# A third raw weight buffer from the gates to the first products, and operand sums in two column parts, in a streaming encoder step

## The chip, the cores and the metric

The kernel runs on one core of one Trainium2 chip. The metric is the device time of one execution in microseconds (us). Engines are named as in the profile: PE (TensorE, matrix products), ACT (ScalarE), DVE (VectorE), POOL (GpSimd), and SP (SyncE), which only issues DMAs. Each engine works through its own instructions in order and waits on semaphores that the others raise. The on-chip memory SBUF has 128 partitions; a tile "128 x n" has n columns on each.

## The reference

One layer on 1056 tokens (1024 prompt, 32 sample), model width 1024, in float32:

```python
h = rms_norm(x, g_mix)
q, k, v, ch, cb, cc, ga, gb = jnp.split(h @ w_in, SPLITS, axis=-1)
a = attn_core(q, k, v) @ w_attn_out                  # windowed attention
bo = (cb * causal_conv3(cc * ch)) @ w_conv_out       # gated short convolution
x = x + (jax.nn.sigmoid(ga) * a + jax.nn.sigmoid(gb) * bo) @ w_mix_out
x = x + memory_attention(rms_norm(x, g_cross) @ w_cq) @ w_co
x = x + jnp.square(jax.nn.relu(rms_norm(x, g_mlp) @ w_up)) @ w_down
y = rms_norm(x, g_final)
```

## The kernel before

Activations lie transposed, features on partitions, tokens on columns, in three chunks `CH` of 384, 384 and 288 tokens; the MLP works on two halves of `HT` = 528 tokens, each of two quarters of `QT` = 264. Every float32 product is three PE products: both operands are split into a high part (fp32r) and a rest, and hi x hi, hi x lo and lo x hi are added (`gemm`, `product`). `split` makes the high part on ACT and the rest on DVE.

**Weights.** `fetch_w` (L147) issues on SP the DMA of a 512 KB weight into a raw tile `wr`, of which there are two; `issue_w` (L158) splits it into `wh` and `wl`. In the gates a dictionary `third` is filled at pair 1 (L933) and cleared at the last pair (L936); while it is filled, each third fetch takes a further raw tile, `wr3`, out of the pool `gtop`, which is open in the gates alone.

**Weight sums.** Gates and MLP use seven products for a 2 x 2 block product instead of eight, which needs sums of weight blocks. POOL makes them in 50 pieces (`pieces`, L692): `sum_step` (L702) loads the next piece from DRAM and then adds the blocks of the piece before in four `tensor_tensor` operations (L719) and stores it to `gsum_d`, `wsum_d` or `usum_d`. Two tiles take turns: `ws` (L700, pool `W["pool"]`, one buffer) and `xacc`. Calls of `sum_step` are placed in the program's order among the attention and output-projection steps. The last piece, a part of `usum_d`, is in `ws`.

**Gates.** `gate_pair(f)` (L908), f from 1 to 7, takes four weights: w_in column 34+f, two sums of `gsum_d` (fetched as `g_sum`), and w_in column 42+f. Its products are 12 matmuls of 384 columns each (3 x 4 row blocks), and for some f a further 24 of 288 columns (`gate_c2`). The first needs only w_in 34+f; the third, `t2`, needs `g_sum` (f-1, 0); the next, `n1`, needs `g_sum` (f-1, 1).

**The stretch after the gates.** Output projections and cross attention of each chunk run as a list of 48 `fillers` (L1648 on): projections of chunk 2, then the first MLP products `up_one` (quarter by quarter, `NQ` row groups) and `up_two` (both quarters). Dictionary `at` hangs further steps behind a filler by its number (`then`, L1657). `up_one` and `up_two` put their results in tiles from `lslot` (L1262, tag `lt`, six buffers; `us`/`uh` with two each for the first three) and store them to `s1_d` and `op_d["b11"]` one step later (`put`, `flush`).

`normed(c, f)` (L1281) computes the MLP's normalised input on DVE and stores it to DRAM (`xn_d`). The operands of the second half of the products are sums of it: n3 = b12 - b22, t2 = b11 - n3, n1 = b11 - b12, n4 = b21 - t2, where the b are quarters of features by halves of tokens. Before, `open_sums` (L1233) loads the parts known by then into the tiles `comb`, `normed(2, f)` adds the columns of chunk 2 by DMA, `sums_first` and `sums_then` (L1377, L1390) compute the sums over all 528 columns into other tiles, three of the four results go by DMA from SBUF to SBUF into `comb`, and `comb_split` (L1397) splits n1, n3 and n4 there at the start of the second half (`up_start`, `up_pair`).

An order of instructions on each engine is made by a scheduler from the program's order and a timeline of its own; instructions under `pin` keep the program's order.

Of the kernel before, what the change touches and what calls it, by code (L numbers as in the profile page):

```python
# [10 lines left out]
F32 = mybir.dt.float32  # L11
# [7 lines left out]
P = 128  # L19
# [4 lines left out]
NF = 8  # L24
# [16 lines left out]
def hybrid_step(ctx: ExitStack, tc: tile.TileContext, io):  # L41
# [37 lines left out]

    ao_d = [[dram.tile([P, 2, n], F32, name=f"ao_d{c}_{kv}") for kv in range(KV)] for c, (_, n) in enumerate(CH)]  # L80
    bc_d, m1_d = spill("bc_d"), spill("m1_d")
    xn_d = [dram.tile([P, NF, HT], F32, name=f"xn_d{h}") for h in range(2)]

    op_d = {k: dram.tile([P, 16, HT], F32, name=f"{k}_d") for k in ("b11", "b21", "b22", "n1", "n3", "t2", "n4")}
    s1_d = dram.tile([P, 16, HT], F32, name="s1_d")
# [61 lines left out]
    def fetch_w():  # L147
        if third:
            third["n"] += 1
        if third and third["n"] % 3 == 0:  # L150
            raw = third["pool"].tile([P, 1024], F32, tag="wr3", name=nm("wr3"))
        else:
            raw = wp.tile([P, 1024], F32, tag="wr", bufs=2, name=nm("wr"))
        src = weight(worder[wpos[0] + len(fetched)])
        sp.dma_start(raw.rearrange("p (i c) -> p i c", i=4) if len(src.shape) == 3 else raw, src)
        fetched.append(raw)
# [751 lines left out]
    def gate_pair(f):  # L908
# [109 lines left out]
    def after_gates():  # L1018
        nonlocal m_cm, mpool, cr_cm, cr
        assert not pieces and "new" not in W  # L1020
        closed(x_cm)
        closed(W["cm"])
# [198 lines left out]
    def open_first():  # L1221

        closed(m_cm)
        S["l"] = ctx.enter_context(tc.tile_pool(name="first", bufs=6, reuse_waits="tile"))
        S["z"] = ctx.enter_context(tc.tile_pool(name="second", bufs=8, reuse_waits="tile"))
        for f in range(NF):
            z = zslot()
            xa[1][f] = (quarter(z, 0), quarter(z, 1))
            sp.dma_start(xa[1][f][1].bitcast(F32)[:, : CH[0][1] - QT], xn_d[0][:, f, QT : CH[0][1]])
        for name in ("w_cq", "w_co"):  # L1230
            del kept[name, 1]

    def open_sums():  # L1233
        closed(cr_cm)
        closed(Y["cm", 1])
        S["s"] = ctx.enter_context(tc.tile_pool(name="sums", bufs=8, reuse_waits="tile"))
        for kind in ("t2", "n1", "n3", "n4"):
            for k in range(4):
                comb[kind, k] = tuple(slot(S["s"], kind, HT) for _ in range(2))
        n = CH[1][0] + CH[1][1] - HT  # L1240
        for k in range(4):
            sp.dma_start(raw("t2", k), xn_d[0][:, k])
            sp.dma_start(raw("n1", k)[:, :n], xn_d[1][:, k, :n])
            sp.dma_start(raw("n3", k)[:, :n], xn_d[1][:, k + 4, :n])
            sp.dma_start(raw("n4", k), xn_d[0][:, k + 4])

    def open_late():
        closed(Y["cm"])
        L["cm"], L["pool"] = opened("late", bufs=1, reuse_waits="tile")

# [18 lines left out]
    quarters = lambda t: t.rearrange("p (q t) -> p q t", q=2)  # L1269


    def in_halves(c):
        o, n = CH[c]
        for h in range(2):
            a, b = max(o, HT * h), min(o + n, HT * h + HT)
            if a < b:
                yield h, slice(a - HT * h, b - HT * h), slice(a - o, b - o)

    xa = [[None] * NF for _ in range(2)]

    def normed(c, f):  # L1281
        t = tmp(CH[c][1])
        pin(dve.scalar_tensor_tensor(t, x1[c][f], col(G_MLP + f), R[c], op0=ALU.mult, op1=ALU.mult))
        for h, to, at in in_halves(c):
            if c < 2 or f > 3:
                sp.dma_start(xn_d[h][:, f, to], t[:, at])
# [83 lines left out]
    def second_b22():  # L1370
        for k in range(4):
            comb["b22", k] = tuple(slot(S["b"], "b22", HT) for _ in range(2))
            sp.dma_start(raw("b22", k), xn_d[1][:, k + 4])

    t2s = {}

    def sums_first(k):  # L1377
        if k == 1:
            n3, n1 = (L["pool"].tile([P, 1024], F32, tag=t, name=nm(t))[:, :HT] for t in ("s31", "s24"))
        else:  # L1380
            n3, n1 = xacc[0][:, :HT], xacc[0][:, HT:]
        t2 = t2s[k] = L["pool"].tile([P, 1024], F32, tag="wr2", bufs=2, name=nm("t2"))[:, :HT]
        pin(dve.tensor_sub(n3, raw("n1", k), raw("n3", k)))
        sp.dma_start(raw("n3", k), n3)
        pin(dve.tensor_sub(t2, raw("t2", k), n3))
        pin(dve.tensor_sub(n1, raw("t2", k), raw("n1", k)))
        sp.dma_start(raw("n1", k), n1)
        pin(act.copy(comb["t2", k][0], t2))

    def sums_then(k):  # L1390
        t2 = t2s.pop(k)
        hi, lo = comb["t2", k]
        pin(dve.tensor_sub(lo, t2, hi.bitcast(F32)))
# [79 lines left out]
    def up_pair(i):  # L1473
# [82 lines left out]
    def dslots(kind, k):  # L1556
        if KINDS.index(kind) % 2 == 0:
            tag = ("t2", "n1", "n3", "b22")[k // 4]
            pool = S["b" if tag == "b22" else "s"]
            return tuple(slot(pool, tag, HT) for _ in range(2))  # L1560
        if k < 4:
            return tuple(slot(S["s"], "n4", HT) for _ in range(2))
        if k < 8:
            return tuple(zslot() for _ in range(2))
        if k < 11:
            return tuple(lslot(F32R) for _ in range(2))
        return tuple(slot(S["h"], "H", HT) for _ in range(2))

# [10 lines left out]
    def open_down():  # L1579
        flush()  # L1580
        closed(L["cm"])
        closed(L["cm2"])
        S["h"] = ctx.enter_context(tc.tile_pool(name="hpool", bufs=10, reuse_waits="tile"))


    def cross_units(c):
# [102 lines left out]
    then(37, call(xacc_tile))  # L1689
    for f in (0, 4, 1, 5, 2, 6, 3, 7):  # L1690
        then(37, call(normed, 2, f))
# [12 lines left out]
    def up_start():  # L1704
# [267 lines left out]
```

## Time and profile before

| | us |
|---|---|
| median of three runs (lowest, highest) | 1788.23 (1781.94, 1788.44) |
| the profiled execution: time | 1787.72 |
| the profiled execution: span from first to last instruction | 1785.9 |
| PE busy in it | 1738.8 |
| POOL busy in it | 584.3 |
| granted TensorE clock, mean | 0.99 |

The profile's page gives the busy time of each engine and a picture of the span in 40 slices. Views of the trace give single stretches: instructions in order of time (start, length, engine, line, operation, output tile, input tiles), groups of equal instructions, waits with what ended them, and DMAs with the time from issue to landing. "SPq" and "POOLq" are the issuing queues. A PE matmul's shown length overlaps the next one's; the distance of two starts is what a matmul costs.

### The profile page before, as it was taken

Reading aid. Unit: us, or ns where it says so; the run is one execution under the profiler, and the core shown is the slowest. Engines: PE = TensorE matmul, PEld = TensorE weight load, DVE = VectorE, ACT = ScalarE, POOL = GpSimd, SP = SyncE. Lnnn points to the kernel's source line nnn. Section 1 sums busy time; section 2 is a strip of 40 time slices with the busy share of each in tenths; the row PEclk is TensorE's granted clock in tenths of the full one; section 3 lists DMA queues with packets and bytes.
Section 4 is the critical chain, followed back from the end, with each engine's and each line's share of the span. In section 5 each row is a group of like instructions: output and inputs, shape, how many; then the busy total and the mean of one; then the engine's idle time right before and its main releaser. Section 6 shows DMA issues by size and latency. Waiting matters only on the chain. (4 is left out here: it accounts for less than half of the span.)

```text
span 1785.9 us, 32537 instructions
## 1 busy us (share of the span) xinstructions
PE 1738.8 (97%) x12250; PEld 1717.8 (96%) x12250; DVE 1181.0 (66%) x2229; ACT 852.5 (48%) x1646; POOL 584.3 (33%) x655
## 2 busy tenths in 40 slices
PE   8999999999999999999999997998999999999998
PEld 8999999999999999999999897988999999999998
DVE  7776867868666737546676866567666686556575
ACT  8643534435345334334565754654444463333443
POOL 0025365643453444532224130014555510000121
PEclk9999999999999999999999998999999999999999
DMA  5333334334346888768765666685666686554554
GB/s 181 107 119 128 111 128 154 130 140 136 138 151 239 284 292 284 262 212 275 253 205 200 226 212 201 215 298 187 229 220 221 215 299 210 185 183 165 197 174 156
DMA packets 185820, 353.64 MB, mean 198 GB/s; under 512 B 20144, under 2 KB 104912, under 8 KB 185536
## 3 DMA queue, kind: packets, MB, share of 16 engines
q1 hardware_dynamic: 170608, 298.98, 49.3%
q0 software_dynamic: 15056, 52.60, 8.3%
q8 instruction: 96, 1.57, 0.3%
q14 instruction: 60, 0.49, 0.1%
HBM read 252.30 MB, written 94.19 MB: 194 GB/s over the span
## 5 line engine op out<-in xcount | busy, mean ns | idle before, releaser
L129 ACT CAST wh<-wr 128x1024 fp32r<-128x1024 f32 x225 | 236.3, 1050 | 435.8 <-PE acc L1758 126.2
L130 DVE TENSOR_TENSOR wl<-wr,wh 128x1024 fp32r<-128x1024 f32 x225 | 293.1, 1303 | 153.1 <-ACT wh L129 152.1
L193 PE MATMUL acc<-X,wh 128*128 128x384 f32 (+1 forms) x864 | 281.8, 326 | 7.6 <-ACT wh L129 7.6
L194 PE MATMUL acc<-X,wh 128*128 128x384 f32 (+1 forms) x864 | 279.1, 323 | 0.0
L195 PE MATMUL acc<-X,wl 128*128 128x384 f32 (+1 forms) x864 | 278.4, 322 | 0.2 <-DVE wl L130 0.2
L269 POOL TENSOR_TENSOR xacc<-xacc,ct 128x384 f32<-128x384 f32 (+1 forms) x56 | 74.6, 1335 | 404.6 <-ACT ct L267 402.7
L193 PEld LDWEIGHTS acc<-X,wh 128*128 128x128 f32 x864 | 162.9, 189 | 8.3 <-ACT wh L129 7.6
L194 PEld LDWEIGHTS acc<-X,wh 128*128 128x128 f32 x864 | 163.1, 189 | 0.6
L195 PEld LDWEIGHTS acc<-X,wl 128*128 128x128 f32 x864 | 162.8, 188 | 0.8 <-DVE wl L130 0.8
L193 PE MATMUL acc<-Y,wh 128*128 128x384 f32 (+1 forms) x432 | 139.8, 325 | 3.2 <-ACT wh L129 3.1
L195 PE MATMUL acc<-Y,wl 128*128 128x384 f32 (+1 forms) x432 | 140.0, 325 | 1.8 <-DMA wl<-wl_d 1.4
L194 PE MATMUL acc<-Y,wh 128*128 128x384 f32 (+1 forms) x432 | 140.0, 325 | 0.3 <-DVE Y L775 0.2
L1758 PE MATMUL acc<-n,wh 128*128 128x264 f32 x352 | 100.0, 284 | 0.0
L1759 PE MATMUL acc<-n,wl 128*128 128x264 f32 x352 | 100.0, 284 | 0.0
L1757 PE MATMUL acc<-n,wh 128*128 128x264 f32 x352 | 100.0, 284 | 0.0
L129 ACT CAST PTh<-pt 128x512 fp32r<-128x512 f32 (+3 forms) x94 | 46.0, 516 | 111.6 <-PE pt L582 110.8
L719 POOL TENSOR_TENSOR ws<-ws 128x256 f32<-128x256 f32 x100 | 93.5, 935 | 5.6
L719 POOL TENSOR_TENSOR xacc<-xacc 128x256 f32<-128x256 f32 x100 | 87.6, 876 | 5.6 <-DMA xacc<-in_w_in 0.3
L193 PEld LDWEIGHTS acc<-Y,wh 128*128 128x128 f32 x432 | 81.6, 189 | 3.8 <-ACT wh L129 3.4
L195 PEld LDWEIGHTS acc<-Y,wl 128*128 128x128 f32 x432 | 81.6, 189 | 2.5 <-DMA wl<-wl_d 1.7
L194 PEld LDWEIGHTS acc<-Y,wh 128*128 128x128 f32 x432 | 81.8, 189 | 0.8 <-DVE Y L775 0.8
L865 PE MATMUL acc<-n,wh 128*128 128x264 f32 x256 | 73.1, 286 | 1.4 <-DVE n L1301 1.3
(404 smaller groups left out, 5502.2 us busy)
## 6 DMA issues: line engine op xcount, KB each, us to landing
wr<-in_w_in SPq DMA_DIRECT2D x53, 512.0 KB, 4.0
wr<-in_w_up SPq DMA_DIRECT2D x52, 512.0 KB, 4.3
wr<-wsum_d SPq DMA_DIRECT2D x40, 512.0 KB, 3.4
wr<-in_w_conv_out SPq DMA_DIRECT2D x24, 512.0 KB, 4.3
wr<-in_w_mix SPq DMA_DIRECT2D x24, 512.0 KB, 4.1
wr<-in_w_down SPq DMA_DIRECT2D x24, 512.0 KB, 4.1
wl<-wl_d SPq DMA_DIRECT2D x18, 512.0 KB, 4.6
n_d<-Z SPq DMA_DIRECT2D x32, 264.0 KB, 4.1
```

Of the source, the lines that this page charges most:

```text
L129: act.copy(hi, src)
L130: dve.tensor_sub(lo, src, hi.bitcast(F32))
L193: pe.matmul(out, wh[:, a], hi, start=(k == 0), stop=False)
L194: pe.matmul(out, wh[:, a], lo, start=False, stop=False)
L195: pe.matmul(out, wl[:, a], hi, start=False, stop=(k == len(acts) - 1))
L269: pool_e.tensor_tensor(acc, acc, sq, op=ALU.add)
L719: pin(pool_e.tensor_tensor(t[:, to], t[:, x], t[:, y], op=ALU.add))
L865: pe.matmul(acc, wh[:, a], lo, start=False, stop=False, skip_group_check=True)
L1757: pe.matmul(a, wh[:, s], hi, start=(t == 0 and k == 0), stop=False, skip_group_check=True)
L1758: pe.matmul(a, wh[:, s], lo, start=False, stop=False, skip_group_check=True)
L1759: pe.matmul(a, wl[:, s], hi, start=False, stop=(t == 1 and k == 7), skip_group_check=True)
```

## The change

- The third raw buffer is now the tile `ws` of the pool `W["pool"]`, which stays open to the end; `third` is filled at gate pair 1 as before and cleared only in `open_late`, so each third fetch uses it from the gates to the first MLP products.
- `xn_d` is one tensor; `normed` of chunk 2 keeps its result in SBUF (`top`).
- The operand sums are made in two column parts: `sums_early` on the first `HA` = 240 columns (tokens of chunk 1), `sums_first` and `sums_then` on the last 288, the latter straight from the outputs of `normed`. Each part is split straight into the operand tiles; the DMAs from SBUF to SBUF and the splits of n1, n3 and n4 in the second half go.
- `lt` has four buffers instead of six, `us`/`uh` one instead of two, `H` in the down projection twelve instead of ten; seven row groups instead of six go through `up_one`; several steps hang at other fillers.

```diff
-    xn_d = [dram.tile([P, NF, HT], F32, name=f"xn_d{h}") for h in range(2)]
+    xn_d = dram.tile([P, NF, NT], F32, name="xn_d")
...
-            raw = third["pool"].tile([P, 1024], F32, tag="wr3", name=nm("wr3"))
+            raw = W["pool"].tile([P, 4, 256], F32, tag="ws", name=nm("wr3")).rearrange("p q c -> p (q c)")
...
-    W["cm"], W["pool"] = opened("wsum", bufs=1, reuse_waits="tile")
+    W["pool"] = ctx.enter_context(tc.tile_pool(name="wsum", bufs=1, reuse_waits="tile"))
...
         if f == 1:
-            third.update(n=2, pool=Y["top"])
+            assert not pieces and "new" not in W
+            third["n"] = 2
             fetch_w()
-        if f == NF - 1:
-            third.clear()
...
-        S["l"] = ctx.enter_context(tc.tile_pool(name="first", bufs=6, reuse_waits="tile"))
+        S["l"] = ctx.enter_context(tc.tile_pool(name="first", bufs=4, reuse_waits="tile"))
...
-            sp.dma_start(raw("n1", k)[:, :n], xn_d[1][:, k, :n])
-            sp.dma_start(raw("n3", k)[:, :n], xn_d[1][:, k + 4, :n])
+            sp.dma_start(raw("n1", k)[:, :HA], xn_d[:, k, HT : HT + HA])
+            sp.dma_start(raw("n3", k)[:, :HA], xn_d[:, k + 4, HT : HT + HA])
...
     def open_late():
+        third.clear()
         closed(Y["cm"])
...
         if c == 2:
-            sp.dma_start(raw("n1" if f < 4 else "n3", f % 4)[:, HT - CH[c][1] :], t)
+            top[f] = t
...
-                s, h = (cr.tile([P, QT], F32, tag=t, bufs=2, name=nm(t)) for t in ("us", "uh"))
+                s, h = (cr.tile([P, QT], F32, tag=t, name=nm(t)) for t in ("us", "uh"))
...
+    def comb_part(kind, k, at, x):
+        hi, lo = comb[kind, k]
+        pin(act.copy(hi[:, at], x))
+        return lambda: pin(dve.tensor_sub(lo[:, at], x, hi[:, at].bitcast(F32)))
+
+    def sums_early(k):
+        at = slice(0, HA)
+        n3, t2, n1, n4 = (tmp(HA) for _ in range(4))
+        pin(dve.tensor_sub(n3, raw("n1", k)[:, at], raw("n3", k)[:, at]))
+        pin(dve.tensor_sub(t2, raw("t2", k)[:, at], n3))
+        pin(dve.tensor_sub(n1, raw("t2", k)[:, at], raw("n1", k)[:, at]))
+        pin(dve.tensor_sub(n4, raw("n4", k)[:, at], t2))
+        for low in [comb_part(kind, k, at, x) for kind, x in (("n3", n3), ("t2", t2), ("n1", n1), ("n4", n4))]:
+            low()
...
     def sums_first(k):
...
-        pin(dve.tensor_sub(n3, raw("n1", k), raw("n3", k)))
-        sp.dma_start(raw("n3", k), n3)
-        pin(dve.tensor_sub(t2, raw("t2", k), n3))
-        pin(dve.tensor_sub(n1, raw("t2", k), raw("n1", k)))
-        sp.dma_start(raw("n1", k), n1)
-        pin(act.copy(comb["t2", k][0], t2))
+        n3, t2 = late["n3", k], late["t2", k]
+        b12, b22 = top.pop(k), top.pop(k + 4)
+        pin(dve.tensor_sub(n3, b12, b22))
+        pin(dve.tensor_sub(t2, raw("t2", k)[:, LATE], n3))
+        pin(dve.tensor_sub(b12, raw("t2", k)[:, LATE], b12))
+        for low in [comb_part("t2", k, LATE, t2), comb_part("n1", k, LATE, b12)]:
+            low()
 
     def sums_then(k):
-        pin(pool_e.tensor_tensor(t2, raw("n4", k), t2, op=ALU.subtract))
-        sp.dma_start(raw("n4", k), t2)
+        n3, t2 = late["n3", k], late["t2", k]
+        pin(dve.tensor_sub(t2, raw("n4", k)[:, LATE], t2))
+        for low in [comb_part("n3", k, LATE, n3), comb_part("n4", k, LATE, t2)]:
+            low()
...
-        if i == 0:
-            comb_split("n4")
...
-    NQ = 6
+    NQ = 7
...
-        then(21, call(second_split, f))
+        then(22, call(second_split, f))
...
-    for i, (_, calls) in zip((23, 24, 26, 27, 29, 30, 31), cross_units(2)):
+    for i, (_, calls) in zip((23, 25, 26, 28, 29, 31, 32), cross_units(2)):
...
-    then(32, call(open_sums))
-    then(33, lambda: item(do_co(2, 0), ("w_co", 0)))
-    then(34, lambda: item(do_co(2, 1), ("w_co", 1)))
-    then(35, call(open_late), call(chunk_col, 2))
-    then(36, call(chunk_row, 2))
+    then(33, call(open_sums))
+    then(34, lambda: item(do_co(2, 0), ("w_co", 0)))
+    then(35, lambda: item(do_co(2, 1), ("w_co", 1)))
     for k in range(4):
-        then(39 + k, call(sums_first, k), *([call(sums_then, k - 1)] if k else []))
+        then(34 + k, call(sums_early, k))
+    then(36, call(open_late), call(chunk_col, 2))
+    then(37, call(chunk_row, 2))
+    then(38, call(late_tiles))
+    for k in range(4):
+        then(38 + k, call(normed, 2, k), call(normed, 2, k + 4), call(sums_first, k))
+        then(43 + k, call(sums_then, k))
...
-    then(43, call(sums_then, 3), call(up_second, 0))
-    then(44, call(comb_split, "n1"))
+    then(43, call(up_second, 0))
...
-        comb_split("n3")
```

More of the change, by code (lines that the diff above doesn't have):

```diff
@@ L1021, in after_gates @@
         closed(x_cm)
-        closed(W["cm"])
         xacc_tile()
@@ L1228, in open_first @@
             xa[1][f] = (quarter(z, 0), quarter(z, 1))
-            sp.dma_start(xa[1][f][1].bitcast(F32)[:, : CH[0][1] - QT], xn_d[0][:, f, QT : CH[0][1]])
+            sp.dma_start(xa[1][f][1].bitcast(F32)[:, : CH[0][1] - QT], xn_d[:, f, QT : CH[0][1]])
         for name in ("w_cq", "w_co"):
@@ L1239, in open_sums @@
                 comb[kind, k] = tuple(slot(S["s"], kind, HT) for _ in range(2))
-        n = CH[1][0] + CH[1][1] - HT
         for k in range(4):
-            sp.dma_start(raw("t2", k), xn_d[0][:, k])
-            sp.dma_start(raw("n1", k)[:, :n], xn_d[1][:, k, :n])
-            sp.dma_start(raw("n3", k)[:, :n], xn_d[1][:, k + 4, :n])
-            sp.dma_start(raw("n4", k), xn_d[0][:, k + 4])
+            sp.dma_start(raw("t2", k), xn_d[:, k, :HT])
+            sp.dma_start(raw("n1", k)[:, :HA], xn_d[:, k, HT : HT + HA])
+            sp.dma_start(raw("n3", k)[:, :HA], xn_d[:, k + 4, HT : HT + HA])
+            sp.dma_start(raw("n4", k), xn_d[:, k + 4, :HT])
     def open_late():
+        third.clear()
         closed(Y["cm"])
@@ L1269, in hybrid_step @@
     quarters = lambda t: t.rearrange("p (q t) -> p q t", q=2)
[L1272 to L1277, printed above, removed]
+    HA = CH[2][0] - HT
+    top = {}
     xa = [[None] * NF for _ in range(2)]
@@ L1283, in normed @@
         pin(dve.scalar_tensor_tensor(t, x1[c][f], col(G_MLP + f), R[c], op0=ALU.mult, op1=ALU.mult))
-        for h, to, at in in_halves(c):
-            if c < 2 or f > 3:
-                sp.dma_start(xn_d[h][:, f, to], t[:, at])
+        o, n = CH[c]
+        if c < 2 or f > 3:
+            sp.dma_start(xn_d[:, f, o : o + n], t)
         if c == 1:
@@ L1372, in second_b22 @@
             comb["b22", k] = tuple(slot(S["b"], "b22", HT) for _ in range(2))
-            sp.dma_start(raw("b22", k), xn_d[1][:, k + 4])
-    t2s = {}
-    def sums_first(k):
[L1378 to L1382, printed above, removed]
-        pin(dve.tensor_sub(n3, raw("n1", k), raw("n3", k)))
-        sp.dma_start(raw("n3", k), n3)
-        pin(dve.tensor_sub(t2, raw("t2", k), n3))
-        pin(dve.tensor_sub(n1, raw("t2", k), raw("n1", k)))
-        sp.dma_start(raw("n1", k), n1)
-        pin(act.copy(comb["t2", k][0], t2))
@@ L1390, in sums_then @@
-    def sums_then(k):
-        t2 = t2s.pop(k)
-        hi, lo = comb["t2", k]
-        pin(dve.tensor_sub(lo, t2, hi.bitcast(F32)))
-        pin(pool_e.tensor_tensor(t2, raw("n4", k), t2, op=ALU.subtract))
-        sp.dma_start(raw("n4", k), t2)
+            sp.dma_start(raw("b22", k), xn_d[:, k + 4, HT:])
+    def comb_part(kind, k, at, x):
[11 more added lines that the diff above has]
+            low()
@@ new lines, in hybrid_step, with late_tiles @@
+    late = {}
+    LATE = slice(HA, HT)
+    def late_tiles():
+        n = HT - HA
+        x = xacc_tile()
+        tiles = [x[:, i * n : i * n + n] for i in range(3)]
+        tiles += [L["pool"].tile([P, n], F32, tag=f"late{i}", name=nm("late")) for i in range(3)]
+        late.update(((kind, k), tiles.pop(0)) for k in range(3) for kind in ("n3", "t2"))
+    def sums_first(k):
+        if k == 3:
+            late.update(((kind, k), tmp(HT - HA)) for kind in ("n3", "t2"))
+        n3, t2 = late["n3", k], late["t2", k]
[5 more added lines that the diff above has]
+            low()
@@ L1564, in dslots @@
             return tuple(zslot() for _ in range(2))
-        if k < 11:
+        if k < 10:
             return tuple(lslot(F32R) for _ in range(2))
@@ L1582, in open_down @@
         closed(L["cm2"])
-        S["h"] = ctx.enter_context(tc.tile_pool(name="hpool", bufs=10, reuse_waits="tile"))
+        S["h"] = ctx.enter_context(tc.tile_pool(name="hpool", bufs=12, reuse_waits="tile"))
     def cross_units(c):
```

3 lines of the change are left out of this document (removed).

## The prediction

> **What bounds the kernel now.** I read the page first (engine shares, the slices, the clock), then stretches of the span one by one, then single engines where a stretch was thin.
>
> ```profile
> span 1785.9 us, 32537 instructions
> ...
> PE 1738.8 (97%) x12250; PEld 1717.8 (96%) x12250; DVE 1181.0 (66%) x2229; ACT 852.5 (48%) x1646; POOL 584.3 (33%) x655
> ...
> PE   8999999999999999999999997998999999999998
> ...
> PEclk9999999999999999999999998999999999999999
> ```
>
> PE is the bound in nearly every slice; apart from the first and the last only the 25th (1072 to 1116 us) and the 28th (1206 to 1250) are thin. So a part of the change pays only where PE waits today, and costs only where PE is made to wait. The stretches that the change touches:
>
> ```profile
> core 0: us, PE busy (x) PEld busy (x) DVE busy (x) ACT busy (x) POOL busy (x), PEclk, DMA share, GB/s
> 667.00:799.30 132.30, 130.54 (x803) 129.57 (x802) 80.04 (x110) 53.90 (x89) 62.87 (x73) 1.00 0.74 252
> 1075.00:1095.00 20.00, 13.58 (x60) 10.36 (x59) 10.12 (x26) 8.18 (x17) 0.00 (x0) 0.74 0.64 210
> 1194.80:1235.00 40.20, 30.22 (x195) 27.86 (x194) 31.20 (x37) 16.92 (x27) 11.47 (x7) 0.87 0.63 234
> ```
>
> The first row is the gates after their first 36 products and one 288-wide block: PE is busy throughout. The other two are the thin ones: 60 and 195 matmuls where a full rate of one every 0.12 us (264 columns, rows below) or 0.13 us (288 columns) would need at most 60 x 0.13 = 7.8 us and 195 x 0.12 = 23.4 us. So 12.2 and 16.8 us, 29 us together, are lost there. That is all that the change can win outside the gates.
>
> ```profile
> 1077.05 0.28 PE L864 MATMUL acc<-Z,wh 128*128 128x264 f32 x1
> 1077.17 0.28 PE L865 MATMUL acc<-Z,wh 128*128 128x264 f32 x1
> ...
> 1093.45 0.30 PE L193 MATMUL acc<-Y,wh 128*128 128x288 f32 x1
> 1093.59 0.30 PE L194 MATMUL acc<-Y,wh 128*128 128x288 f32 x1
> ```
>
> **The change, part 1: the third raw buffer in the gates.** The third weight buffer was a tile of its own; now it is the tile `ws`, in which POOL adds up weight pieces (`sum_step`). The assertion at the first gate pair says that all pieces have been handed out by then. That is true of the order in which the program is written. On the chip POOL is far behind that order:
>
> ```profile
> 666.55 0.53 POOL L714 DMA_DIRECT2D xacc<-in_w_down  x1 [3.81 <-DMA wsum_d<-xacc]
> ...
> 721.33 0.54 POOL L714 DMA_DIRECT2D ws<-in_w_down  x1 [4.00 <-DMA wsum_d<-ws]
> 721.89 3.19 POOL L719 TENSOR_TENSOR xacc<-xacc 128x256 f32<-128x256 f32 x4
> 725.49 0.57 POOL L725 DMA_DIRECT2D wsum_d<-xacc  x1 [0.41 <-POOL xacc L719]
> 728.85 1.46 POOL L712 DMA_DIRECT2D xacc<-in_w_up  x2 [2.78 <-DMA wsum_d<-xacc]
> ...
> 768.08 1.45 POOL L712 DMA_DIRECT2D ws<-in_w_up  x2 [7.01 <-DMA usum_d<-ws]
> 769.55 3.19 POOL L719 TENSOR_TENSOR xacc<-xacc 128x256 f32<-128x256 f32 x4
> 773.14 1.47 POOL L723 DMA_DIRECT2D usum_d<-xacc  x2 [0.41 <-POOL xacc L719]
> 774.63 5.15 POOL L719 TENSOR_TENSOR ws<-ws 128x256 f32<-128x256 f32 x4
> 780.19 1.45 POOL L723 DMA_DIRECT2D usum_d<-ws  x2 [0.41 <-POOL ws L719]
> ```
>
> The last piece leaves `ws` only after 780.19. But SP fetches the first third-buffer weight, `g_sum` (0, 1), at 657.58, and PE uses it from 667.03:
>
> ```profile
> 657.58 0.32 SPq L155 DMA_DIRECT2D wr<-gsum_d  x1
> ```
>
> ```profile
> 657.52 0.34 PE L864 MATMUL acc<-X,wh 128*128 128x384 f32 x1
> ...
> 666.86 0.33 PE L866 MATMUL acc<-X,wl 128*128 128x384 f32 x1
> 667.03 0.33 PE L864 MATMUL acc<-X,wh 128*128 128x384 f32 x1
> ```
>
> The built order of SP's instructions shows the new wait. Before (first line), the fetch needs one of POOL's DMA counters; after, all eight and POOL's own, at the counts that are reached with the last of POOL's 138 DMAs, the store of `usum_d` out of `ws`:
>
> ```
> 239 L155 DMACopy wr_1321_7908<-gsum_d 128x1024 [waits DMAHW0_49,DMASW1_49,PE_49]
> 251 L155 DMACopy wr_1321_7907<-gsum_d 128x1024 [waits DMASW4_49,DMASW5_49,DMASW3_49,DMASW6_49,DMASW2_49,DMASW7_49,DMASW1_49,DMAHW4_49,DMASW0_49,Pool_49]
> ```
>
> SP issues in order, so all weights of the later pairs, the loads of `a_d` and the stores of `m1_d` stand behind this wait. PE's built order still begins with the same 36 products and the 24-matmul block (657.52 to 667.03), then needs this weight. So PE stops at 667.0. It starts again when POOL is done, the fetch has landed and ACT has made its high half.
>
> When is POOL done? From the load at 666.55 nine load intervals lead to that at 768.08: six of 512 KB pieces to 728.85 (mean 10.4 us), three more of `w_up` pieces. With SP silent and DVE out of work nothing slows POOL, so I take the fastest step seen, 721.33 to 728.85: 0.54 issue, 3.19 four adds, 0.41, 0.57 store issue, 2.78 for the store to land = 7.5 us. The first interval I leave at 9, since SP's last transfers still run: 9 + 5 x 7.5 = 46.5, to 713.1. The next, with two load issues, takes 7.5 + 0.9 = 8.4; the other two, with two store issues as well, 9.6 each: 740.7. Then the last steps, 1.45 + 3.19 + 0.4 + 1.47 + 3.19 + 0.4 + 1.45 = 11.6: 752.3.
>
> ```profile
> wr<-in_w_in SPq DMA_DIRECT2D x14, 512.0 KB, 3.6
> ...
> wsum_d<-xacc POOLq DMA_DIRECT2D x7, 512.0 KB, 3.1
> ```
>
> ```profile
> wr<-gsum_d SPq DMA_DIRECT2D x12, 512.0 KB, 4.8
> ...
> usum_d<-ws POOLq DMA_DIRECT2D x4, 256.0 KB, 5.0
> ```
>
> ```profile
> 661.19 1.05 ACT L129 CAST wh<-wr 128x1024 fp32r<-128x1024 f32 x1 [0.89 <-DMA wr<-gsum_d]
> ```
>
> The first fence holds landings (size, median us) in the calm stretch 340 to 545, the second in the crowded 660 to 790, the third ACT's cast of one weight. Calm ones hold here: 752.3 + 3.1 + 0.3 issue + 3.6 + 1.1 for ACT = 760.4. PE idles 93.4 us. Bounds: the first interval at 7.5 too gives 92, and half a microsecond off each of nine steps, an estimate for a chip with nothing else to do, 88; POOL at today's pace gives 780.19 + 1.45 + 5.0 + 0.3 + 4.8 + 1.1 = 792.8, or 126.
>
> A rule of the Trainium skill bears on the pace: "SBUF — State Buffer", Who interferes with whom, says that a VectorE instruction with two SBUF inputs and a GpSimd instruction that reads SBUF exclude each other. The rows agree that POOL's adds vary (3.19 for four at 721.89, 5.15 at 774.63). By that rule the idle DVE gives POOL the short adds; with the long ones in each of the eleven sums left, the sum would be up to 22 us higher.
>
> PE then restarts at a lowered clock. After a 3 us wait in this trace matmuls stood 0.24 us apart instead of 0.14, until 4.1 us after the restart:
>
> ```profile
> 1089.08 0.61 PE L193 MATMUL acc<-Y,wh 128*128 128x288 f32 x1 [3.12 <-ACT wh L129]
> ...
> 1092.43 0.45 PE L194 MATMUL acc<-Y,wh 128*128 128x288 f32 x1
> 1092.67 0.45 PE L195 MATMUL acc<-Y,wl 128*128 128x288 f32 x1
> ```
>
> That costs 2 us. The rest of the gates then runs without POOL's traffic. Its 792 matmuls (552 of 384 columns, 0.173 apart at 666.86; 240 of 288) need 127 of the 132.3 us, so at most 5 can come back; I take 2.
>
> **Part 2: the buffer kept to the first products, operand sums in two parts.** The buffer lets the second `w_cq` fetch move ahead of the 24 issues of the `normed` outputs of chunk 1 in SP's order; `second_split` comes one filler later. Both answer to waits in 1075 to 1095. The sums take the three splits n1, n3, n4 out of the start of the second half:
>
> ```profile
> L1301 DVE TENSOR_TENSOR n<-n,n 128x528 fp32r<-128x528 f32 x12 | 13.2, 1142 | 0.0
> ```
>
> ```profile
> PE acc L865 <- DVE t L1393: 4.1, 1, 4.1
> PE acc L193 <- ACT wh L129: 3.1, 1, 3.1
> PE pc L864 <- ACT b L1300: 2.8, 1, 2.8
> ```
>
> The first fence is the group of these twelve splits in 1185 to 1235 (busy us, mean ns), the second PE's waits (total, times, longest) from 1060 to 1240. So 13.2 us of DVE leave a stretch where DVE is busy 31 of 40 us, and with them twelve DMAs that carried n1, n3 and n4 into their operand tiles and eight that carried `normed` outputs of chunk 2 there; the same number of columns (8 x 528 a row group, the n4 difference moved from POOL to DVE among them) is worked earlier, where DVE has room (PE bounds there), or right behind `normed`. I take about half of the 29 us: 15. Against it stand fewer slots: `lt` six to four, `us`/`uh` two to one. An `up_one` takes 24 x 0.12 = 2.9 us, uses two slots, and its stores are issued at the next one:
>
> ```profile
> s_d<-lt SPq DMA_DIRECT2D x9, 132.0 KB, 3.0
> b_d<-lt SPq DMA_DIRECT2D x9, 132.0 KB, 4.5
> ```
>
> With four slots they are wanted back 5.8 us later and land after 2.9 + 3.0 to 4.5, up to 1.6 late; for nine items 14 us at worst, when nothing else stands between them. Cross attention does stand between most: I take 4. Net -11, bounds -29 and +14.
>
> **Sum.** 1785.9 + 93.4 + 2 - 2 - 11 = 1868.3 span. The profiled execution took 1787.72, 1.8 around its span: 1870. It lies 0.5 under the median of the three runs, which I leave out.
>
> **Rivals.** *The buffer is free in time* (faster): were POOL's sums over before 657.6, part 2 alone would count: 1788 - 11 = 1777, down to 1759. The skill's "Trainium Kernel Development and Optimization", Best Practices, asks for double buffering to overlap DMA with compute, and a deeper one would point this way; the row of 667 to 799 shows PE busy for 130.5 of 132.3 us, so there is hardly a wait for a weight to remove there. For it: the program's order. Against it: the POOL rows, 123 us too late. 4%. *POOL keeps its pace*: if its steps are slow by themselves and not by SP's traffic, 126 instead of 93.4: 1903. Against it the step at 721.33, with SP active even; for it the mean of 10.4. 10%. *The slots bite*: part 2 ends at +14: 1895. For it the landings above, against it the units between. 12%. My forecast: 74%, by itself 1850 to 1892.
>
> **Numbers.** The range 1850 to 1895 leaves out the first rival, most of the second and the forecast's thin ends, about 2 in 10. Faster by over 0.5% (9 us, about what these runs can tell): 0.04; within: 0.01; slower: 0.95.
>
> **What would show it.** One wait of PE of 85 to 105 us after about 36 products of the gates, ended by ACT's `wh` after a fetch into `wr`; SP silent from about 672 to 756; POOL's last `usum_d` store near 752; load intervals near 7.5 us; PEclk low for one slice after it. In 1194 to 1235 (some 82 us later) no L1301 on `n`, and fewer than 17 us lost. I am wrong if SP goes on during POOL's sums, or if PE has other products to do then.

## The result, and the profile after

| | before | after |
|---|---|---|
| median us (lowest, highest; 4 runs each) | 1787.83 (1781.94, 1788.44) | 1853.21 (1852.28, 1854.56) |
| ratio to before, 95% interval | | 1.0374 [1.0351, 1.0397] |
| span of the profiled execution | 1785.9 | 1850.8 |
| granted TensorE clock, mean | 0.99 | 0.971 |

The changed kernel is 65 us slower. The page of the changed kernel, the lines that answer to those of before:

```profile
span 1850.8 us, 32562 instructions
...
PE 1727.6 (93%) x12250; PEld 1713.2 (93%) x12250; DVE 1180.8 (64%) x2270; ACT 853.8 (46%) x1660; POOL 567.9 (31%) x651
...
PE   8999999999999940699999999999999999999998
...
PEclk9999999999999975799999999999999999999999
```

There is one hole, in the 15th to 17th of the 40 slices (648 to 787 us). Everything else is as full as before or fuller: the thin 25th and 28th slices have gone. PE is busy for 11 us less than before at the same 12250 matmuls. The hole, first as PE shows it (start, length, engine, line, operation, what ended the idle time), then as SP and POOL do:

```profile
666.73 0.34 PE L866 MATMUL acc<-X,wl 128*128 128x384 f32 x1
758.42 0.69 PE L864 MATMUL acc<-X,wh 128*128 128x384 f32 x1 [91.36 <-ACT wh L129]
...
760.67 0.52 PE L864 MATMUL acc<-X,wh 128*128 128x384 f32 x1
760.99 0.52 PE L865 MATMUL acc<-X,wh 128*128 128x384 f32 x1
...
763.77 0.34 PE L864 MATMUL acc<-Y,wh 128*128 128x384 f32 x1
763.95 0.34 PE L865 MATMUL acc<-Y,wh 128*128 128x384 f32 x1
```

```profile
669.33 1.52 SPq L799 DMA_DIRECT2D ct<-bc_d  x3
753.77 7.34 SPq L155 DMA_DIRECT2D wr<-gsum_d  x3
```

```profile
676.14 0.53 POOL L714 DMA_DIRECT2D ws<-in_w_down  x1 [4.65 <-DMA wsum_d<-ws]
676.69 3.13 POOL L719 TENSOR_TENSOR xacc<-xacc 128x256 f32<-128x256 f32 x4
...
683.55 0.53 POOL L714 DMA_DIRECT2D xacc<-in_w_down  x1 [2.75 <-DMA wsum_d<-xacc]
...
749.98 1.45 POOL L723 DMA_DIRECT2D usum_d<-ws  x2 [0.41 <-POOL ws L719]
```

SP issues nothing from 670.85 (669.33 + 1.52) to 753.77, 2.3 us after POOL's last store out of `ws` has been issued (749.98 + 1.45). Then it issues the fetch of `g_sum`, and 4.65 us later PE runs. POOL meanwhile works alone, one load interval of `w_down` in 683.55 - 676.14 = 7.41 us.

How much of the hole comes back later? I added up the matmuls of stretches of 10 us in both traces and compared the times at which the same count was reached (a matmul across a border counts twice, so these counts run to 12 600 and not 12 250):

| matmuls done | 4250 | 4500 | 5250 | 6750 | 7250 | 7750 | 8000 | 9000 | 12000 |
|---|---|---|---|---|---|---|---|---|---|
| before, us | 638.6 | 677.1 | 797.0 | 1039.7 | 1121.5 | 1184.5 | 1229.6 | 1349.9 | 1705.1 |
| after, later by | 0.0 | 93.8 | 91.1 | 91.6 | 78.6 | 80.0 | 65.1 | 63.0 | 63.4 |

In the rest of the gates 2.7 us come back (93.8 to 91.1). Between the counts 6750 and 9000 it is 28 us, of which 26.5 in two steps before count 8000; behind that nothing does. The three stretches between the counts 6750, 7250, 7750 and 8000, first of before and then of after (busy us and count of each engine, granted clock, share of the DMA engines, GB/s):

```profile
1039.70:1121.50 81.80, 70.85 (x492) 66.39 (x491) 51.41 (x99) 41.52 (x83) 10.92 (x9) 0.92 0.62 208
1121.50:1184.50 63.00, 61.49 (x488) 60.59 (x487) 36.91 (x74) 40.51 (x100) 5.55 (x5) 0.97 0.63 221
1184.50:1229.60 45.10, 36.33 (x248) 34.23 (x247) 31.81 (x37) 22.23 (x38) 13.20 (x8) 0.89 0.74 268
```

```profile
1131.30:1200.10 68.80, 64.17 (x489) 63.41 (x489) 52.28 (x99) 40.55 (x78) 11.03 (x9) 0.98 0.71 239
1200.10:1264.50 64.40, 61.33 (x488) 60.61 (x487) 48.17 (x118) 44.78 (x120) 4.39 (x4) 0.97 0.65 227
1264.50:1294.60 30.10, 29.83 (x243) 29.40 (x242) 23.30 (x38) 18.72 (x37) 6.38 (x4) 1.00 0.56 188
```

The first and the third are the ones with the thin slices. Over the three rows together the time falls by 189.9 - 163.3 = 26.6 us. PE's idle time (length less PE busy) falls from 21.2 to 8.0, and PE's busy time for the same products from 168.7 to 155.3. So one half of the gain is waits that are gone. The other half is busy time, for two reasons. Fewer matmuls run at the lowered clock (granted clock 0.92 and 0.89 before, 0.98 and 1.00 after); an estimate from the rows, length times the share of the clock that was not granted, is at most 13.4 us lost before and 3.3 after. And a matmul that stands alone is shown at its full length (0.39 us at 1078.20, the next start 0.47 later), while in a dense row it overlaps the next one (0.28 us at 1077.05, the next start 0.12 later).

### The profile page after: what moved, and what is told of

It is laid out like the page before. It is cut to its first block, busy times and chain, and to the rows that moved or that the text cites. A ratio compares the mean times of both kernels' runs of the same rounds, so it can differ in the third digit from the quotient of the medians.

```text
span 1850.8 us, 32562 instructions
## 1 busy us (share of the span) xinstructions
PE 1727.6 (93%) x12250; PEld 1713.2 (93%) x12250; DVE 1180.8 (64%) x2270; ACT 853.8 (46%) x1660; POOL 567.9 (31%) x651
## 4 chain that ended last, share of the span: by engine, by line
PE 81%; DMA 8%; POOL 5%; DVE 2%; issue 2%; ACT 1%; SPq 0%; DVEq 0%; ACTq 0%; POOLq 0%
PE acc L193 10%; PE acc L195 10%; PE acc L194 10%; PE acc L1768 6%; PE acc L1770 6%; PE acc L1769 6%; PE acc L864 6%; PE acc L866 6%; PE acc L865 6%; DMA wsum_d<-xacc 2%; DMA wsum_d<-ws 2%; POOL ws L719 2%; POOL xacc L719 2%; PE pc L865 2%; PE pc L866 2%
## 5 line engine op out<-in xcount | busy, mean ns | idle before, releaser
L193 PEld LDWEIGHTS acc<-X,wh 128*128 128x128 f32 x864 | 163.1, 189 | 8.3 <-ACT wh L129 7.7
L194 PEld LDWEIGHTS acc<-X,wh 128*128 128x128 f32 x864 | 163.4, 189 | 0.6
L864 PE MATMUL acc<-X,wh 128*128 128x384 f32 x112 | 38.3, 343 | 91.4 <-ACT wh L129 91.4
L864 PEld LDWEIGHTS acc<-X,wh 128*128 128x128 f32 x112 | 21.5, 192 | 91.7 <-ACT wh L129 91.7
L1769 PE MATMUL acc<-n,wh 128*128 128x264 f32 x352 | 100.2, 285 | 0.0
L1768 PE MATMUL acc<-n,wh 128*128 128x264 f32 x352 | 100.2, 285 | 0.0
L1049 POOL TENSOR_TENSOR ct<-ct,ct 128x384 f32<-128x384 f32 (+1 forms) x21 | 23.1, 1100 | 233.4 <-DMA wr<-in_w_conv_out 142.6
L719 POOL TENSOR_TENSOR ws<-ws 128x256 f32<-128x256 f32 x100 | 86.0, 860 | 5.6
L719 POOL TENSOR_TENSOR xacc<-xacc 128x256 f32<-128x256 f32 x100 | 83.8, 838 | 5.5 <-DMA xacc<-in_w_in 0.2
```

Of the source, the lines that this page charges most:

```text
L193: pe.matmul(out, wh[:, a], hi, start=(k == 0), stop=False)
L194: pe.matmul(out, wh[:, a], lo, start=False, stop=False)
L719: pin(pool_e.tensor_tensor(t[:, to], t[:, x], t[:, y], op=ALU.add))
L864: pe.matmul(acc, wh[:, a], hi, start=(start and k == 0), stop=False, skip_group_check=True)
L1768: pe.matmul(a, wh[:, s], hi, start=(t == 0 and k == 0), stop=False, skip_group_check=True)
L1769: pe.matmul(a, wh[:, s], lo, start=False, stop=False, skip_group_check=True)
```

## The experiments

The theory after the result: the alias with `ws` costs the wait of 91 us and nothing else; the rest of the change wins some 28 us. Rivals are that the gain and the stall belong together (queues that ran ahead during the hole), and that some third thing in the gates costs too. What is called the first stretch below is matmuls 6750 to 7250, the second one 7750 to 8000.

| kernel | median us (lowest, highest) | ratio to before, 95% | later than before at 5250 | first stretch | second stretch |
|---|---|---|---|---|---|
| before | 1787.4 to 1788.7 in five sets | | 0 | 81.8 | 45.1 |
| after | 1853.2 (1852.3, 1854.6) | 1.0374 [1.0351, 1.0397] | 91.1 | 68.8 | 30.1 |
| e1 own tile, `ws` at the last pair | 1774.4 (1771.9, 1775.2) | 0.9917 [0.9904, 0.9930] | 14.7 | 67.2 | 34.0 |
| e2 alias alone | 1882.9 (1880.9, 1884.3) | 1.0525 [1.0511, 1.0539] | 92.7 | 80.1 | 45.7 |
| e3 own tile, gates only | 1773.5 (1768.1, 1779.9) | 0.9916 [0.9897, 0.9934] | 2.8 | 75.9 | 32.4 |
| e5 last piece in `xacc` | 1847.0 (1846.1, 1848.5) | 1.0328 [1.0313, 1.0344] | 87.0 | 67.6 | 32.0 |
| e7 `ws` after the gates | 1775.2 (1765.5, 1779.1) | 0.9914 [0.9890, 0.9938] | 3.8 | 68.6 | 34.3 |
| e6 fewer slots alone | 1787.0 (1784.0, 1790.8) | 0.9989 [0.9980, 0.9998] | 3.5 | 79.6 | 43.7 |
| e4 slots and late `ws` | 1788.7 (1779.0, 1791.3) | 0.9988 [0.9972, 1.0004] | 11.6 | 69.0 | 43.8 |
| e8 `ws` from the fillers | 1777.5 (1773.7, 1778.7) | 0.9939 [0.9923, 0.9954] | 12.5 | 68.9 | 34.1 |
| e9 slots, `ws` from the fillers | 1789.7 (1784.3, 1792.3) | 1.0006 [0.9994, 1.0018] | 12.2 | 70.9 | 42.9 |
| e12 `ws` tied to late data | 1766.2 (1761.3, 1769.3) | 0.9874 [0.9854, 0.9893] | -0.1 | 70.7 | 34.4 |
| e10 new tile from first products | 1772.9 (1769.8, 1779.2) | 0.9921 [0.9904, 0.9939] | 2.5 | 72.4 | 33.5 |

The last three columns are of the profiled execution, in us.

### First set: where the 91 us and the 28 us belong

**e1**, on the changed kernel:

```diff
-            raw = W["pool"].tile([P, 4, 256], F32, tag="ws", name=nm("wr3")).rearrange("p q c -> p (q c)")
+            raw = third_raw()
...
-            third["n"] = 2
+            third.update(n=2, pool=Y["top"])
             fetch_w()
+        if f == NF - 1:
+            third["pool"] = W["pool"]
```

`third_raw` takes `ws` where the pool is `W["pool"]`, else a tile `wr3` of the pool given. Pair `NF - 1` is the last, f = 7; the expectations count it from 0 and call it the eighth.

> The changed kernel, but in the gates the third buffer has a tile of its own, as before, and it becomes `ws` only at the last gate pair (the eighth); everything from the first products on is as changed. Theory (the wait on POOL's last sum is worth 91, part 2 a gain of about 28): PE has no wait over 5 us in the gates, SP fetches through them, the span is 1851 - 91 = 1760, the time about 1762, 0.986 of before. Rival 1 (the sums cost as well because a third buffer of any kind crowds the DMA engines): a good part of the 91 stays. Rival 2 (part 2 gained only because POOL and SP had run dry behind the wait, or because the order around it was shifted): the stall goes and so does the gain, time 1785 to 1790. If the eighth pair's fetch still comes before POOL's last store, up to 10 us of a wait is left.

Measured 1774, not 1762, though the large wait is gone. The late gain is nearly whole (14.6 us in the first stretch, 11.1 in the second), so rival 2 falls as far as it needs the large wait. A smaller one is left, the wait named last, and only e12 has the gain without any. SP's queue in e1, and POOL's last store:

```profile
755.09 0.33 SPq L160 DMA_DIRECT2D wr<-in_w_in  x1
782.01 0.33 SPq L160 DMA_DIRECT2D wr<-in_w_conv_out  x1
```

```profile
778.00 1.45 POOL L728 DMA_DIRECT2D usum_d<-ws  x2 [0.41 <-POOL ws L724]
```

SP is silent for 27 us and goes on 2.6 us after the end of that store's issue; PE waits for `wh` twice, 12.5 us in all.

**e2**, on the kernel of before:

```diff
-            raw = third["pool"].tile([P, 1024], F32, tag="wr3", name=nm("wr3"))
+            raw = W["pool"].tile([P, 4, 256], F32, tag="ws", name=nm("wr3")).rearrange("p q c -> p (q c)")
...
-            third.update(n=2, pool=Y["top"])
+            third["n"] = 2
```

> The kernel of before with one thing of the change: in the gates the third raw buffer is `ws`; it ends at the eighth pair as before, and operand sums and slots are as before. Theory: PE stops after the first products of the second pair and starts again about 91 us later, +91 and nothing else: 1788 + 91 = 1879 (1870 to 1890), ratio 1.051. Rival (the wait in the changed kernel comes from the two parts together): the time is under 1850.

Its waits of PE in the gates (us in total, times, longest):

```profile
PE acc L864 <- ACT wh L129: 91.3, 1, 91.3
```

1883, +94 us, and both late stretches as before. The alias alone makes the loss. Little of it comes back, and the hole alone does not bring the late gain.

**e3**, on the changed kernel: the raw tile is `third["pool"].tile(... tag="wr3")` as before, filled with `Y["top"]` at pair 1 and cleared at the last pair.

> The changed kernel with the third buffer as before: a tile of its own, in the gates alone. The operand sums in two parts and the fewer slots stay. It tells how much of part 2's 28 us is the sums' and how much the buffer's after the gates. If the sums have all: as the first run, about 1762. If the buffer kept to the first products has the part at the waits between 1075 and 1095 (12.2 us lost there): about 1772 to 1775. If the sums gain nothing: about 1788.

1773.5, the second of the three: the sums (with the fewer slots) bring 15 us, 12.7 of them in the second stretch. In the first stretch a wait is back that the changed kernel and e1 do not have (PE, time order):

```profile
1088.24 0.61 PE L193 MATMUL acc<-Y,wh 128*128 128x288 f32 x1 [5.89 <-ACT wh L129]
```

**e5**, on the changed kernel: `if n % 2 == 0: return xacc_tile()` in `sum_tile`, so that the last piece is in `xacc`.

> The changed kernel with the two tiles of the weight sums exchanged: the last piece is summed in `xacc`, the one before it in `ws`. If PE waits for the last store out of `ws` and nothing else, the fetch starts when the last but one piece is stored. In the last steps that is some 5 to 10 us earlier (one piece: 3.1 of adds and 1.5 to 2.9 of store issue and landing): 1843 to 1848, PE's wait 82 to 86. Rival (the wait is for POOL's whole work, or for its DMA counters as a set): 91 us of wait and 1853, no difference.

Wait 86.6 us (0.6 over the range given), time 1847.0, 6.2 below the changed kernel. Its POOL and SP:

```profile
745.82 1.47 POOL L723 DMA_DIRECT2D usum_d<-ws  x2 [0.41 <-POOL ws L719]
...
750.85 1.45 POOL L723 DMA_DIRECT2D usum_d<-xacc  x2 [0.41 <-POOL xacc L719]
```

```profile
749.44 7.29 SPq L155 DMA_DIRECT2D wr<-gsum_d  x3
```

The fetch follows the store out of `ws` by 2.2 us and goes before POOL's last one. It is that tile that SP waits for, not POOL as a whole.

### Second set: what the buffer is worth behind the gates

**e7**, on e1: `third.clear()` at pair `NF - 1`, and `third.update(n=2, pool=W["pool"])` in `after_gates`.

> As the first run, but the third buffer has its own tile through all of the gates and is given up at the eighth pair, as before; after the last gate pair it is taken up again as `ws`. In the first run one wait was left: its 5250th matmul came 14.7 us later than before (its wait on `wh` is 12.5 us), and from there on it won 26 to 28. Theory (that wait is POOL's last store again, and the late gain does not need it): 1774 - 12 = 1762, 0.985 of before. Rival (what is won late is what was lost in the gates: queues that ran ahead during a wait): 1774, no difference to the first run.

The profiled execution took 1765.5, the median is 1775. The rival has the median, the theory the profile. In the profile POOL's last store was issued at 768.24, some 10 us sooner than in e1, and SP was silent for only 17.7 us, to 772.24; PE waited 0.5 us. Which run meets which case no median can tell, hence e8 and e12.

**e6**, on the kernel of before: `first` with `bufs=4`, `us`/`uh` without `bufs=2`, `hpool` with `bufs=12`, `k < 10`.

> The kernel of before with only the fewer slots: `lt` four in place of six, `us`/`uh` one in place of two, the H pool and its map as in the changed kernel; operand sums and third buffer as before. The prediction's price was +4, bounds 0 and +14: 1793 (1788 to 1802). Since the changed kernel won all of the 28 us that were to be had, the theory now is 0 to +2: 1788 to 1791. Rival: +10 and more, so that the sums would have won more than the stretch had.

1787.0, ratio 0.9989: the slots cost nothing.

**e4**, on e6: `W["pool"]` stays open, `third_raw` and the `third.update` of e7, and `third.clear()` in `open_late`.

> The run before with one thing added: after the gates the third raw buffer goes on as `ws`, up to the late pool; operand sums as before. It tells what the buffer after the gates is worth where the sums are as they were. From the two runs with the sums (first and third of the other set, matmuls 6750 to 7250: 14.6 us won with the buffer, 6.0 without) the theory says 6 to 9 us below the run before, some 1780 to 1785. Rival (the buffer wins only where the sums have moved, or nothing): within 2 us of the run before.

1788.7, no gain, so the rival by the time. But the profiled execution, at 1783.9 faster than the median, shows two effects against each other: it is 11.6 us late at count 5250 (e6: 3.5; one wait of PE for `wh` is 9.4 us), and its first stretch is 10.6 us shorter than in e6.

### Third set: the loss in the last gate pairs

**e8** and **e9**, on e7 and e4: the `third.update` moves from `after_gates` to the second filler.

```diff
-        third.update(n=2, pool=W["pool"])
...
-    then(1, call(chunk_stats, 1))
+    then(1, call(lambda: third.update(n=2, pool=W["pool"])), call(chunk_stats, 1))
```

> As the run with `ws` after the gates, but the third buffer is taken up again as `ws` only with the second filler of the first products (some 100 us after POOL's last store) and not right after the gates. In that run the profiled execution took 1765.5 and the others up to 1779; in the two runs with the same early use the matmuls 5000 to 5250 came 11.5 to 12 us late, after a silence of SP that ended 2 to 5 us after POOL's last `usum_d` store was issued. Theory (the spread is that race between POOL and SP, and the late gain needs the buffer from the fillers on alone): median 1765 (1761 to 1770), about 0.987 of before, and SP silent for no more than 9 us in the last gate pairs, as before. Rival (the spread has another source): 1774 again.

> The run with the slots and the late buffer (operand sums as before), with the buffer taken up as in the run beside it. There its profile had lost 11 us to POOL's last store and won 12 of them back in the matmuls 6750 to 7250. Theory (the buffer is worth something by itself where SP's weight fetches stand behind other issues): 1787 less 5 to 9, 1778 to 1782. Rival (it wins back only what a delay left over): 1786 to 1788, as with the slots alone.

Both theories fell: 1777.5 and 1789.7, and again 12 us late at 5250. So no run here has the late buffer with the old sums and without a delay before it, and what it is worth there stays open. The buffer was not meant to be in use in the last gate pairs, and yet SP waits. Its queue in e8 says why:

```profile
752.91 0.33 SPq L160 DMA_DIRECT2D wr<-in_w_in  x1
778.74 0.33 SPq L160 DMA_DIRECT2D wr<-in_w_cq  x1
779.17 0.38 SPq L160 DMA_DIRECT2D wr<-in_w_in  x1
...
780.11 0.67 SPq L160 DMA_DIRECT2D wr<-gsum_d  x1
```

The first fetch after the silence is a `w_cq` of cross attention in chunk 1; in e12, below, it is issued at about 960, some 180 us later. The built order of SP's instructions in e8 has it as the 295th, in front of the `w_in` and `g_sum` of the last gate pairs:

```
295 L160 DMACopy wr3_2055_11303<-in_w_cq 128x1024 [waits DMASW4_49,DMASW5_49,DMASW3_49,DMASW6_49,DMASW2_49,DMASW7_49,DMASW1_49,DMAHW0_49,DMASW0_49,Pool_49]
296 L160 DMACopy wr_1524_8974<-in_w_in 128x1024 [waits DMAHW1_49,DVE_49]
```

It waits for POOL's last sum and its DMAs. That it was put there at all says that the scheduler's timeline has that sum done by then; the timeline itself is not shown. On the chip POOL is later, and SP, which issues in order, stands still with the gates' weights behind it.

### Fourth set: the fetch tied to later data

**e12**, on e8:

```diff
-    then(1, call(lambda: third.update(n=2, pool=W["pool"])), call(chunk_stats, 1))
+    then(1, call(third_late), call(chunk_stats, 1))
...
+    def third_late():
+        t = W["pool"].tile([P, 4, 256], F32, tag="ws", name=nm("wr3"))
+        act.copy(t[:, 0, :1], x1[1][NF - 1][:, :1])
+        third.update(n=2, pool=W["pool"])
```

> As the run with `ws` from the fillers on, with a one-column ACT copy from the last row group of chunk 1 into `ws` ahead of its first use as a weight buffer. In that run SP's first fetch after its silence (778.74, 2 us after POOL's last `usum_d` store) was the `w_cq` that belongs to the fillers: the order of SP's instructions had it already in the gates, where nothing but POOL's last sum held it, and `g_sum` and `a_d` stood behind it. The copy gives it a later predecessor, so it stands where the changed kernel has it. Theory: SP is silent for no more than 9 us in the last gate pairs, PE has no 8.6 us wait there, the late gain stays (matmuls 6750 to 7250 in some 69 us, 7750 to 8000 in some 34): 1777 - 9 to 12 = 1765 to 1768, 0.988, with a narrower spread. Rival (the late gain hangs on a delay before it): 1774 and more.

**e10**, on e7: `wsum` is closed in `after_gates` as before, and `open_first` opens a pool for the third buffer and fills `third`.

> The third buffer as in the run beside it, but no `ws`: a tile of its own again, opened where the first products' slots are opened, on memory of the conv and mix tiles. The second `w_cq` fetch of chunk 2 then does not move ahead of the `normed` outputs in SP's order (526th, in the changed kernel 508th). Theory (it is this move that takes the wait on `wh` away, 5.9 us in the run without a late buffer, and with it 6 to 9 us of the matmuls 6750 to 7250): 1773, as without a late buffer, matmuls 6750 to 7250 in about 75. Rival (any third buffer in the first products does it): 1766, 69.

In e12 that fetch is the 435th. SP's queue:

```profile
757.81 0.33 SPq L160 DMA_DIRECT2D wr<-gsum_d  x1
758.18 0.42 SPq L933 DMA_DIRECT2D ct<-a_d  x1
765.07 0.32 SPq L160 DMA_DIRECT2D wr<-gsum_d  x1
...
773.89 0.33 SPq L160 DMA_DIRECT2D wr<-in_w_in  x1
776.39 0.33 SPq L160 DMA_DIRECT2D wr<-in_w_conv_out  x1
```

No silence over 8.2 us (before: 8.5), nothing lost at 5250, both late stretches short: 1766.2, ratio 0.9874 [0.9854, 0.9893]. It is the fastest of all, 21 us below before and 87 below the changed kernel. Its stretches:

```profile
1040.20:1110.90 70.70, 66.49 (x485) 65.18 (x483) 49.66 (x93) 38.65 (x73) 9.18 (x9) 0.93 0.72 242
...
1174.60:1209.00 34.40, 31.11 (x249) 30.26 (x248) 24.94 (x42) 19.23 (x39) 5.90 (x4) 1.00 0.55 187
```

e10 came out at 1772.9, as e3 without a late buffer did, so the median is the theory's. The profile is not: its first stretch (72.4) is nearer to the rival's number, with waits for `wh` of 2.7 and 1.6 us where e3 had one of 5.9, and only 1.7 us longer than e12's, while the medians are 6.7 apart. That e12's earlier place of the fetch is what makes it faster than e10 is therefore not shown, and why e10's 3.5 us against e3 do not show in the median stays open.

## Why the prediction was right, step by step

The sum was 1870, the time is 1853.2, 3 us above the low end of the range. Part 2 alone was forecast 17 us too small; the other terms were each within 2 us.

**The stall: right, 93.4 against 91.4.** The chain was the one named, link by link: POOL's last store issued to 751.43 (752.3 forecast), landed and seen by SP 2.3 us later (3.1), fetch, landing and cast 4.65 (5.0). POOL's steps took 7.41 (7.5), with two load issues 8.4 (8.4), with two store issues as well 9.2 (9.6, where its own terms give 7.5 + 0.9 + 0.9 = 9.3); the first interval, left at 9, took 9.8 (666.32 to 676.14). That POOL would run faster with SP silent and DVE idle decides this number: at its pace of before the wait would have been 126. The groups of POOL's adds (busy us, mean ns), before from 676 to 780 and after from 676 to 752:

```profile
L719 POOL TENSOR_TENSOR ws<-ws 128x256 f32<-128x256 f32 x20 | 22.6, 1128 | 1.3
L719 POOL TENSOR_TENSOR xacc<-xacc 128x256 f32<-128x256 f32 x20 | 18.3, 917 | 1.3
```

```profile
L719 POOL TENSOR_TENSOR ws<-ws 128x256 f32<-128x256 f32 x20 | 14.5, 724 | 1.3
L719 POOL TENSOR_TENSOR xacc<-xacc 128x256 f32<-128x256 f32 x20 | 14.5, 723 | 1.3
```

The same forty adds take 29.0 us in place of 40.9, so 12 of the 30 us by which POOL's last store came sooner (780.19 to 749.98) are adds, and the rest is mainly loads and stores that land sooner (the `wsum_d` stores after 2.9 us at the median, in place of 4.3 and 4.8). The Trainium skill, "SBUF — State Buffer", Who interferes with whom, lets a VectorE instruction with two SBUF inputs contend with a GpSimd instruction that reads SBUF. The trace agrees: with DVE idle all forty adds take 724 ns. For the adds e1 tells DVE's part from SP's, since SP is silent there from 755.42 to 782.01 while PE and DVE go on:

```profile
756.84 5.12 POOL L724 TENSOR_TENSOR ws<-ws 128x256 f32<-128x256 f32 x4
...
769.33 3.18 POOL L724 TENSOR_TENSOR xacc<-xacc 128x256 f32<-128x256 f32 x4
...
774.40 3.19 POOL L724 TENSOR_TENSOR ws<-ws 128x256 f32<-128x256 f32 x4
```

Beside the first four, 3.4 of the 5.1 us long, DVE runs instructions that read two SBUF tiles each (`wl<-wr,wh` twice, `ct<-ct,ct`); beside each of the other groups it runs only one, which reads a PE product (`v<-acc,s`, `Gb<-acc,v`). So the adds are slow where DVE runs instructions of the first kind, although SP is silent. The short step that the prediction took (3.19 at 721.89) has SP's transfers under way and DVE idle. SP's silence, one of the two reasons that the prediction gives, does not account for the adds. For the landings the parts of the two aren't told apart.

**The lowered clock after it: right, 2 against 2.4.** Matmuls stood 0.32 apart until 763.55 and 0.18 afterwards. The Trainium skill, "TensorE: Matmul & The Clock Gate", Part 1, has the clock at half after an idle window and at full rate after at least one busy window of about 3.4 us; here the half rate agrees (0.50 granted from 750 to 760), and it lasted 5.1 us, longer than one such window.

The row from which the prediction took this cost was misread. In the kernel of before the clock was lowered from 1083 on, 3 us before the 3.12 us wait began (1085.96 to 1089.08); the same matmul is shown at 0.39 us ahead of it and at 0.59 behind it:

```profile
1081.91 0.39 PE L865 MATMUL acc<-Z,wh 128*128 128x264 f32 x1
...
1083.51 0.59 PE L865 MATMUL acc<-Z,wh 128*128 128x264 f32 x1
```

The granted clock is 1.00 from 1076 to 1083 and 0.50 from 1083 to 1093.15. No wait in the seven us before 1083 is longer than 0.69 us; PE was busy for 4.53 of them. So here several short waits went before the lowered clock, and the row does not show what one wait of 3 us does. The forecast of 2 us needed only that the clock be lowered after the hole.

**The rest of the gates: right, -2 against -2.7** (93.8 at 4500, 91.1 at 5250).

**Part 2: the right sign, the size off.** The step that failed is "I take about half of the 29 us: 15. Against it stand fewer slots: ... I take 4." It measured 28 in the place of 11. The 29 us themselves were right. Halving them was not. The splits over all 528 columns left the thin stretch (before, twelve that took 13.2 us); twelve of 288 columns are left there, from 1255 to 1320:

```profile
L1372 DVE TENSOR_TENSOR n<-ct,n 128x288 fp32r<-128x288 f32 x6 | 2.7, 452 | 0.4 <-ACT n L1371 0.4
...
L1372 DVE TENSOR_TENSOR n<-late,n 128x288 fp32r<-128x288 f32 x3 | 1.4, 452 | 0.4 <-ACT n L1371 0.4
L1372 DVE TENSOR_TENSOR n<-xacc,n 128x288 fp32r<-128x288 f32 x3 | 1.3, 451 | 0.0
```

They take 5.4 us, and e3's second stretch is 32.4 against 45.1. In the first stretch the wait of PE for a `w_cq` weight is gone in the kernels that fetch it earlier, and with each wait went the slow matmuls behind it, which the count against the full rate had in the 29 us already. How the gain parts between the earlier fetch and the other moved steps is not shown. The slots' 4 us were none: e6 alone is at 0.9989 [0.9980, 0.9998]. With the measured terms the sum is 1785.9 + 91.4 + 2.4 - 2.7 - 28.2 = 1848.8; the span is 1850.8, since 0.5 us are lost between the counts 5250 and 6750 and 1.5 behind 12000.

**The rivals.** *The buffer is free in time*: e12 stands in for it, with a tile of its own in the gates and `ws` only when POOL is done with it. It took 1766, within the 1777 to 1759 given for that rival; POOL's 123 us of lateness lay between. *POOL keeps its pace* is refuted by the adds and landings above, *the slots bite* by e6.

Not settled: the changed kernel's second stretch (30.1) is 4 us shorter than in e12, e8, e7 and e1 (34.0 to 34.4), and e12, without a hole, wins 21.8 us in the two stretches where the changed kernel wins 28.0. Whether the hole lets something run ahead there was not tried; e5, with a hole of 87 us, has 32.0 and e3, without one, 32.4.

## What to carry to other kernels

A buffer that is free in the order of the program is free on the chip only when its last user is done there: before sharing it, look up that user's last instruction in the trace and compare it with the first one that would wait. A DMA queue that issues in order makes one such wait everybody's wait, and a scheduler that believes the buffer free can carry the waiting fetch far ahead of where it was written (e8); tie it to data of its own time (e12). Where a thin stretch is to be filled, count it against the full rate of matmuls: idle time alone showed half of what could be won.

## What had not been expected

In e8 and e9 an edit far behind the gates held the gates: a weight that could have been fetched 180 us later made PE wait 8.6 and 9.2 us there. And e7, in which POOL's end and SP's fetch nearly coincide, spreads widely (1765.5 to 1779.1), while the kernels with the long hole agree within 4 us (1852.3 to 1854.6, 1880.9 to 1884.3, 1846.1 to 1848.5). That the race is the cause of the spread is not shown: e10 and e3, which have no such fetch, spread nearly as far (9.4 and 11.9 us), and e1 and e8, which have one, stay within 3.3 and 5.0.
